# Hybrid decoder layer: two buffers for a head's K and Q, a freely issued second output tile, and 1/rms spread by transposes

## The chip, the cores and the metric

The kernel runs on one core of a Trainium2 chip, with TensorE (PE), VectorE (DVE), ScalarE (ACT), GpSimd (POOL) and SyncE (SP, which issues nearly all DMAs). The metric is the device time of one execution in microseconds. Beside the time of several runs there is one execution taken by the hardware profiler, whose instructions are shown here as "the trace"; times in it count from its first instruction.

## The reference

One decoder layer over 2048 positions of width 1024, all in float32, with a final RMSNorm:

```python
u = rmsnorm(h, norm_mix_w)
hq, hf, hi, hg, att = split(u @ w_in)
f = lb + (1 - lb) * sigmoid(hf)                  # 4 heads, key and value width 128
S_t = diag(f_t) S_{t-1} + (1 - f_t) v_t^T;  o_t = S_t^T q_t     # HGRN2
o_hg = rmsnorm(o, hg_norm_w) * silu(hg)
o_att = sliding_window_attention_with_sinks(att + b_attn)       # 8 query heads, 2 kv heads, window 128
h = h + concat(o_hg, o_att) @ w_out
v = rmsnorm(h, norm_ffn_w)
h = h + (silu(causal_conv(v @ w_gate)) * (v @ w_up)) @ w_down   # width 2816, conv of 3 taps
out = rmsnorm(h, final_norm_w)
```

rmsnorm multiplies by 1/sqrt(mean(x^2) + 1e-6), over the 1024 features of a position.

## The kernel before, in words

Features lie on the 128 partitions and positions along the free axis; the 2048 positions are worked in two halves of 1024 (`hf` = 0, 1), each 2 x 512 columns for one PSUM bank. A float32 product with a weight is made of three products of rounded parts, W_hi X_hi + W_hi X_lo + W_lo X_hi (float32r, one pass each; `split` and `prep` make the parts on ACT and DVE). `unit` is one such product of a 128-column block of weights with 8 blocks of X: 8 x 3 x 2 = 48 matmuls of 128x512. Products of float32 operands take two records each.

**Stages of a half.** The input norm and keys and values (kv); then a mixer of four HGRN2 heads (`hgrn`) woven with four attention pairs (`attend`); then `out_proj`, eight output tiles `pop` (d = 0 to 7) over the eight blocks of the mixer's output `M`; then the MLP (`gate_up`, `down`), whose products are saved by a Strassen-like scheme. All eight blocks enter every output tile, in the order 0, 4, 1, 5, 2, 6, 7, 3; blocks 7 and 3 are those of the last attention pair and the last head and come last.

**Order.** Each engine works through its own list of instructions in a fixed order. That order is written when the program is made: the generators of heads and attention are stepped by hand, which gives each instruction a priority, and a planner plays the program through on a modelled timeline, giving each engine the first instruction that is ready there. Tiles of one tag share a fixed number of buffers, and an instruction that needs a buffer waits until the last reader of the old tile is done. `tc.issue_after(ins)` keeps the instructions traced under it behind `ins` on that engine. `marks[m]` holds the last level product of level m, `marks["po"]` the last product of a head's output; `AFTER` says which output tiles are queued behind which mark. Here output tile 1 comes behind the last head's product of level m = 8 and tile 2 behind its po.

**A head.** `f` and `hq` are two units; `q` (named hg in the trace, its slot's name) is hq times 1/rms. K = 1 - f (L431) and Q = q f (L433). `pdiag` (L441) gives the diagonal of the score tile ST; seven levels m = 1 to 64 follow (`plev`, L469 for m < 32, L482 above): a product of Q with a copy G of K (L467), put into ST by L493, and then K and Q are multiplied by the decay of their neighbour (L475, L476, L485, L486), so that each level waits for the one before it. Then K is transposed (`pkn`, L511), `pu` and SS carry the state from block to block (L518, L522), `po` (L536, L537) is the output, with ST, Q and SS, `on` (L545) its norm, `pot` (L550) its transpose back, and the gate `g` is multiplied in. pdiag, plev, pkn, pu, po and pot all use the two PSUM banks of the tag "hg", and ST, Kn and `on` share two buffers of the tag "t4". Of attention pairs, `psc` are scores, `ppt` transposed probabilities, `po`/`pp` on DVE (L395) their masked copies, and `poT` (L403) the products with V; they use the two banks of "at". Units, gates and output tiles use four banks of "mm", output tile 2 those of "at".

The last two heads are stepped into each other: head 2's state and output are traced around the f and q units of head 3, and the levels of head 3 come behind them.

```python
            step(a2, h2, h3, a2, h2, a2)
            step(a3, h3, a3, h2, h3)
            for kt in (0, 4, 1, 5, 2, 6):
                M[kt] = split(mix[kt])
            step(h3, a3, h3, a3)
```

**Norms.** `Stats` adds up squares over the feature blocks in `acc`. `inverse` sums over the partitions by products with a column of ones (`pst`, L238), which leaves the sums of 128 positions in a column, takes 1/sqrt by `rsqrt` (a bit trick and three Newton steps on DVE, L152 to L162), and writes the diagonal of each column into `acc` (L242). `spread` (L252, `pinv`) multiplies that by a square of ones, so that each position's 1/rms stands on all partitions, and ACT copies it into `acc` (L255). The statistics are called invb, sums and acc in the trace after the tiles they lie in. At the very end the last half's first 512 columns are worked in two quarters, and the final products (L981) of both quarters are held behind the last instruction that `inverse` returns.

Of the kernel before, what the change touches and what calls it, by code (L numbers as in the profile page):

```python
# [8 lines left out]
F32 = mybir.dt.float32  # L9
# [4 lines left out]
ALU = mybir.AluOpType  # L14
# [3 lines left out]
P = 128  # L18
D = 1024
KT = D // P  # L20
S = 2048
HALF = 1024
# [3 lines left out]
HG = 4  # L26
# [7 lines left out]
QUADS = ["A11", "A12", "A21", "A22"]  # L34
PRODUCTS = [("P1", "A11", "B11"), ("P5", "S1", "T1"), ("P6", "S2", "T2"), ("P3", "S4", "B22"),
            ("P7", "S3", "T3"), ("P2", "A12", "B21"), ("P4", "A22", "T4")]
AFTER = {1: 8, 2: "po"}
LEVELS = [1, 2, 4, 8, 16, 32, 64]
NEG = -1.0e30
UT = 7  # L40
# [5 lines left out]
def hymba_layer(ctx: ExitStack, tc: tile.TileContext, a: dict, out: bass.AP):  # L46
    nc = tc.nc

    def pool(name, bufs=1, space=None, stack=ctx, **kw):
        if space is not None:  # L50
            kw["space"] = space
        return stack.enter_context(tc.tile_pool(name=name, bufs=bufs, **kw))
# [12 lines left out]
    def ps(kind, name):  # L65
        return spaces[kind].tile([P, 512], F32, tag=kind, name=name)
# [9 lines left out]
    ones = cp.tile([P, P], F32, name="ones")  # L76
# [3 lines left out]
    ident = cp.tile([P, P], F32, name="ident")  # L80
# [65 lines left out]
        nc.vector.tensor_scalar(C.omlb, C.lb, -1.0, 1.0, op0=ALU.mult, op1=ALU.add)  # L146


    def rsqrt(ss, n, scale, keep=None):

        ms = sp.tile([P, n], F32, tag=f"ms{n}", name="ms")
        nc.vector.tensor_scalar(ms, ss, scale, EPS, op0=ALU.mult, op1=ALU.add)  # L152
        y = sp.tile([P, n], F32, tag=f"y{n}{keep}", name="y")
        yi = y.bitcast(I32)
        nc.vector.tensor_scalar(yi, ms.bitcast(I32), 1, None, op0=ALU.logical_shift_right)
        nc.vector.tensor_scalar(yi, yi, -1.0, float(0x5F3759DF), op0=ALU.mult, op1=ALU.add)
        nc.vector.tensor_scalar(ms, ms, -0.5, None, op0=ALU.mult)
        t = sp.tile([P, n], F32, tag=f"t{n}", name="t")
        for _ in range(3):
            nc.vector.tensor_tensor(t, y, y, op=ALU.mult)  # L160
            nc.vector.tensor_tensor(t, t, ms, op=ALU.mult)
            nc.vector.scalar_tensor_tensor(y, t, 1.5, y, op0=ALU.add, op1=ALU.mult)  # L162
        return y

    def raw4(src):
# [5 lines left out]
    def prep(src, slots=False, parts=(slice(0, D),)):  # L171

        raw = raw4(None)
        hi, lo = [hp.tile([P, D], F32R, tag="m", name=f"w{t}", bufs=KT) if slots else
                  wp.tile([P, D], F32R, tag=t, name=f"w{t}", bufs=2) for t in ("hi", "lo")]
        for c in parts:
            nc.sync.dma_start(raw[:, c], src[:, c])
            nc.scalar.copy(hi[:, c], raw[:, c])  # L178
            nc.vector.tensor_tensor(lo[:, c], raw[:, c], hi[:, c].bitcast(F32), op=ALU.subtract)  # L179
        return hi, lo  # L180
# [34 lines left out]
    class Stats:  # L215
# [16 lines left out]
        def inverse(self, keep):  # L232

            n = self.acc.shape[-1]
            nt = n // P
            st = ps("hg", "pst")
            for c in range(nt):
                nc.tensor.matmul(st[:, c:c + 1], self.acc[:, c * P:(c + 1) * P], ones[:, 0:1],  # L238
                                 start=True, stop=True)
            rs = self.rs = rsqrt(st[:, 0:nt], nt, 1.0 / D, keep)  # L240
            dg = self.acc
            return nc.vector.tensor_tensor(dg.rearrange("p (c t) -> p c t", t=P),  # L242
                                    ident.unsqueeze(1).to_broadcast([P, nt, P]),
                                    rs.unsqueeze(2).to_broadcast([P, nt, P]), op=ALU.mult)

        def spread(self, bank=None):

            n = self.acc.shape[-1]
            w = min(n, 512)
            for b in range(n // w):  # L250
                pb = ps(aux[b % 2 if bank is None else bank], "pinv")[:, 0:w]
                nc.tensor.matmul(pb, ones, self.acc[:, b * w:(b + 1) * w], start=True, stop=True)  # L252
                if bank is not None:
                    return pb
                nc.scalar.copy(self.acc[:, b * w:(b + 1) * w], pb)  # L255
# [31 lines left out]
    def across(t, base, dims):  # L287

        v = t[:, :]
        return bass.AP(v.tensor, v.offset + base, [list(v.ap[0])] + dims)  # L290
# [126 lines left out]
    def hgrn(hf, h, X, invb, vs, WG, mix, p, fu=None):  # L417
# [9 lines left out]
            nc.vector.scalar_tensor_tensor(q[:, bs], qu[b], 128.0 ** -0.5, invb[:, bs], op0=ALU.mult, op1=ALU.mult)  # L427
        nc.vector.tensor_scalar(f, f, C.omlb[:, h:h + 1], C.lb[:, h:h + 1], op0=ALU.mult, op1=ALU.add)
        yield
        K = p.tile([P, HALF], F32, tag="K", name="K", bufs=1)  # L430
        nc.vector.tensor_scalar(K, f, -1.0, 1.0, op0=ALU.mult, op1=ALU.add)  # L431
        Q = p.tile([P, HALF], F32, tag="Q", name="Q", bufs=1)
        nc.vector.tensor_tensor(Q, q, f, op=ALU.mult)  # L433


        ST = p.tile([P, TT, P], F32, tag="t4", name="ST", bufs=2)
        for b in range(NB):
            pd = ps("hg", "pdiag")
            for i in range(4):
                c = slice((b * 4 + i) * P, (b * 4 + i + 1) * P)  # L440
                nc.tensor.matmul(pd[:, i * P:(i + 1) * P], K[:, c], q[:, c], start=True, stop=True)  # L441
            nc.vector.tensor_tensor(ST[:, 4 * b:4 * b + 4], pd.rearrange("p (i t) -> p i t", i=4),
                                    ident.unsqueeze(1).to_broadcast([P, 4, P]), op=ALU.mult)


        late = h == HG - 2

        def gate():
            gu = unit(WG.get(h, a["w_g"][h]), X, "g")
            s = p.tile([P, HALF], F32, tag="f", name="sg", bufs=2)  # L450
            t = p.tile([P, HALF], F32, tag="f", name="ug", bufs=2) if late else q
            for b, bs in halves():
                nc.vector.tensor_tensor(blocks(t[:, bs], b), blocks(gu[b]), blocks(invb[:, bs]), op=ALU.mult)
                nc.scalar.activation(s[:, bs], t[:, bs], AF.Sigmoid)
                if late:
                    nc.vector.tensor_tensor(q[:, bs], q[:, bs], t[:, bs], op=ALU.mult)
                nc.vector.tensor_tensor(q[:, bs], q[:, bs], s[:, bs], op=ALU.mult)

        F = f
        for m in LEVELS:  # L460
            nb = HALF // (2 * m)
            pl = ps("hg", "plev")
            if m < 32:
                n, nu = 64 // m, TT // 2
                far, near = [[512 - m, 2], [P, nu], [2 * m, n], [1, m]], [[512 + m, 2], [P, nu], [2 * m, n], [1, m]]
                G = p.tile([P, 512], F32, tag="G", name="G", bufs=2)
                nc.scalar.copy(across(G, 0, [[m, 2], [P, nu], [2 * m, n], [1, m]]), across(K, 0, near))  # L467
                for u in range(nu):
                    marks[m] = nc.tensor.matmul(across(pl, u * 64, [[256, 2], [1, 64]]), G[:, u * P:(u + 1) * P],  # L469
                                                across(Q, u * P + m, [far[0]] + far[2:]), start=True, stop=True)  # L470
                nf = P // m
                Kv, Qv = across(K, 0, near), across(Q, m, far)
                Fk = across(F, 1, [[4 * nf - 1, 2], [nf, nu], [2, n], [0, m]])
# [3 lines left out]
            else:  # L477
                Qv = Q.rearrange("p (b w m) -> p b w m", w=2, m=m)
                Kv = K.rearrange("p (b w m) -> p b w m", w=2, m=m)
                for c in range(TT):  # L480
                    for s0 in range(0, P, 2 * m):
                        nc.tensor.matmul(pl[s0:s0 + m, c * m:(c + 1) * m], K[:, c * P + s0:c * P + s0 + m],  # L482
                                         Q[:, c * P + s0 + m:c * P + s0 + 2 * m], start=True, stop=True)
                Fv = F.rearrange("p (b w) -> p b w", w=2)
# [22 lines left out]
        for b in range(NB):  # L507
            pk = ps("hg", "pkn")
            for i in range(4):
                c = slice((b * 4 + i) * P, (b * 4 + i + 1) * P)  # L510
# [3 lines left out]
        for b in range(NB):  # L514
            pu = ps("hg", "pu")
            for i in range(4):
                c = 4 * b + i
                marks["pu"] = nc.tensor.matmul(pu[:, i * P:(i + 1) * P], Kn[:, c], v[:, c], start=True, stop=True)  # L518
            for i in range(4):
                c = 4 * b + i  # L520
                prev = state[:, h] if c == 0 else SS[:, c - 1]
                nc.vector.scalar_tensor_tensor(SS[:, c], prev, F[:, c:c + 1], pu[:, i * P:(i + 1) * P],  # L522
                                               op0=ALU.mult, op1=ALU.add)
        yield
        g = q
        if h < HG - 2:
            gate()
            yield
        on = p.tile([P, TT, P], F32, tag="t4", name="on", bufs=2)
        ss = p.tile([P, TT], F32, tag="ss", name="ss", bufs=2)  # L530
        po = [ps("hg", "po") for _ in range(NB)]
        for c in range(TT):
# [3 lines left out]
            nc.tensor.matmul(o, ST[:, c], v[:, c], start=True, stop=False)  # L536
            marks["po"] = nc.tensor.matmul(o, Q[:, cs], prev, start=False, stop=True)  # L537
            nc.scalar.activation(on[:, c], o, AF.Square, accum_out=ss[:, c:c + 1])
        rs = rsqrt(ss, TT, 1.0 / P)
        if h == HG - 1:  # L540
            mix[h] = new_x()
# [5 lines left out]
        for b, bs in halves():  # L547
# [5 lines left out]
            else:  # L553
                nc.vector.scalar_tensor_tensor(blocks(g[:, bs]), blocks(pt, b), C.hgw, blocks(g[:, bs]),
                                               op0=ALU.mult, op1=ALU.mult)
# [48 lines left out]
    def out_proj(hf, M, p):  # L604
# [11 lines left out]
        for d in range(KT):  # L616
# [8 lines left out]
            if d >= len(W):  # L625
                W.append(prep(a["w_out"][d]))
            with tc.issue_after(marks[AFTER[d]].ins) if d in AFTER else ExitStack():
                o = unit(W[d], M, "pop", order, "at" if d == 2 else "mm", in_turn=d == KT - 1)
# [363 lines left out]
    for hf in range(NH):  # L992
        X, kv, invb, rs, f0 = nxt
        with ExitStack() as st:
            p = pool(f"mix{hf}", stack=st, reuse_waits="tile")
# [28 lines left out]
        with ExitStack() as st:  # L1024
            p = pool(f"ffn{hf}", stack=st, reuse_waits="tile")
# [65 lines left out]
```

## Time and profile before

| | |
|---|---|
| median of 3 runs | 2217.16 us (2214.91 to 2218.22) |
| the profiled execution | 2213.91 us, its span 2212.2 us |
| mean granted clock of TensorE | 0.995 |
| PE, PEld, DVE, ACT, POOL busy | 98%, 82%, 74%, 47%, 1% of the span |
| instructions | 29221 |
| DMA | 254.15 MB, 115 GB/s in the mean |

PEld is the loading of weights, which runs beside the matmuls. A matmul's record is longer than its share of a row of matmuls, since they are pipelined: the distance from start to start is the pace. A line such as L197 is that of a helper (`unit`); the tile's name says which product it is. In the rows of time, the bracket gives the idle time of the engine before the instruction and what ended it.

### The profile page before, as it was taken

How to read it: one execution, taken by the hardware profiler on the slowest of the kernel's cores; microseconds unless marked ns; L12 is line 12 of the kernel's file. 1: busy time of each engine (PE TensorE's matmuls, PEld its weight loads, DVE VectorE, ACT ScalarE, POOL GpSimd, SP SyncE). 2: the span in 40 equal slices, each digit the busy share in tenths (PEclk: the TensorE clock that was granted, in tenths of full speed). 3: DMA queues.
4: the chain of work that ended last, by engine and by line, in shares of the span. 5: the costliest groups of instructions: out<-in, count | busy, mean ns of one | idle time of the engine just before them, and what ended most of it. 6: DMA issues, size and time to landing. Idle time of an engine off the chain costs nothing.

```text
span 2212.2 us, 29221 instructions
## 1 busy us (share of the span) xinstructions
PE 2175.0 (98%) x11302; PEld 1822.3 (82%) x11302; DVE 1638.0 (74%) x2458; ACT 1049.3 (47%) x1825; POOL 14.4 (1%) x37
## 2 busy tenths in 40 slices
PE   8999998999999999999999999999999999999997
PEld 6988987778888888888889889878788888888887
DVE  6567567688887888775865666667878888887766
ACT  5445454454444445335725455535534444443353
POOL 2000000000000000000000000000000000000000
PEclk9999999999999999999999999999999999999999
DMA  4111112323333234964631111113232323359643
GB/s 154 39 29 39 29 29 77 108 83 93 113 100 115 87 128 145 376 230 159 203 124 38 30 29 39 59 37 136 64 125 86 125 85 119 95 194 393 220 130 128
DMA packets 89995, 254.15 MB, mean 115 GB/s; under 512 B 11008, under 2 KB 13184, under 8 KB 89856
## 3 DMA queue, kind: packets, MB, share of 16 engines
q1 hardware_dynamic: 87552, 251.17, 34.1%
q8 instruction: 88, 1.44, 0.3%
q10 hardware_dynamic: 2304, 1.12, 0.2%
q14 instruction: 51, 0.42, 0.1%
HBM read 195.10 MB, written 57.15 MB: 114 GB/s over the span
## 4 chain that ended last, share of the span: by engine, by line
PE 95%; DVE 3%; ACT 1%; DMA 1%; issue 0%; ACTq 0%; DVEq 0%
PE X L708 7%; PE X L709 7%; PE X L710 7%; PE pop L197 6%; PE q L197 4%; PE hq L197 4%; PE f L197 4%; PE pdx L890 4%; PE pdx L891 4%; PE Y L708 4%; PE pdx L892 4%; PE Y L710 4%; PE Y L709 4%; PE g L197 4%; PE pdy L891 3%; PE pdy L890 3%
## 5 line engine op out<-in xcount | busy, mean ns | idle before, releaser
L585 ACT CAST whi<-raw 128x1024 fp32r<-128x1024 f32 x88 | 92.7, 1053 | 109.7 <-PE X L709 68.8
L709 PE MATMUL X<-T,whi 128*128 128x512 f32 x352 | 137.4, 390 | 0.0
L708 PE MATMUL X<-T,whi 128*128 128x512 f32 x352 | 137.1, 389 | 0.0
L710 PE MATMUL X<-T,wlo 128*128 128x512 f32 x352 | 137.0, 389 | 0.0
L774 DVE SCALAR_TENSOR_TENSOR y<-ga,cw,y 128x1024 f32<-128x1024 f32 x88 | 112.4, 1277 | 28.2 <-ACT y L772 28.1
L714 ACT COPY u<-X 128x512 f32<-128x512 f32 x88 | 51.5, 585 | 122.3 <-PE X L710 122.2
L586 DVE TENSOR_TENSOR wlo<-raw,whi 128x1024 fp32r<-128x1024 f32 x88 | 107.0, 1216 | 0.0
L586 DVE TENSOR_TENSOR xld<-raw,xhd 128x1024 fp32r<-128x1024 f32 x72 | 80.5, 1129 | 18.9 <-ACT xhd L585 18.3
L178 ACT CAST whi<-raw 128x1024 fp32r<-128x1024 f32 (+2 forms) x61 | 62.9, 1035 | 65.9 <-PE hq L197 11.8
L585 ACT CAST xhd<-raw 128x1024 fp32r<-128x1024 f32 x72 | 69.7, 979 | 40.2 <-DMA raw<-act1T 14.4
L197 PE MATMUL pop<-XH,wlo 128*128 128x512 f32 x256 | 83.3, 391 | 0.7 <-DVE wlo L179 0.7
L197 PE MATMUL pop<-XL,whi 128*128 128x512 f32 x256 | 84.0, 392 | 0.0
L197 PE MATMUL pop<-XH,whi 128*128 128x512 f32 x256 | 82.9, 396 | 0.4 <-ACT XH L208 0.2
L179 DVE TENSOR_TENSOR wlo<-raw,whi 128x1024 fp32r<-128x1024 f32 (+2 forms) x61 | 72.9, 1199 | 13.9 <-ACT whi L178 13.9
L708 PEld LDWEIGHTS X<-T,whi 128*128 128x128 f32 x352 | 66.1, 188 | 14.0 <-ACT u L714 0.3
L710 PEld LDWEIGHTS X<-T,wlo 128*128 128x128 f32 x352 | 66.1, 188 | 13.9 <-issue 0.2
L709 PEld LDWEIGHTS X<-T,whi 128*128 128x128 f32 x352 | 66.1, 188 | 13.8 <-issue 0.2
L890 PE MATMUL pdx<-xhd,hid 128*128 128x512 f32 x192 | 74.4, 391 | 1.0 <-ACT hid L585 1.0
L891 PE MATMUL pdx<-xld,hid 128*128 128x512 f32 x192 | 74.8, 390 | 0.0
L708 PE MATMUL X<-T,Sh 128*128 128x512 f32 x176 | 69.0, 392 | 5.2 <-ACT s L714 5.2
L892 PE MATMUL pdx<-xhd,lod 128*128 128x512 f32 x192 | 73.7, 389 | 0.0
L578 PE MATMUL pvv<-whi,XL 128*128 128x256 f32 x256 | 73.2, 287 | 0.0
(363 smaller groups left out, 6544.5 us busy)
## 6 DMA issues: line engine op xcount, KB each, us to landing
wr<-in_w_down SPq DMA_DIRECT2D x90, 512.0 KB, 5.2
raw<-in_w_gate SPq DMA_DIRECT2D x44, 512.0 KB, 3.7
raw<-in_w_up SPq DMA_DIRECT2D x44, 512.0 KB, 3.6
raw<-act0T SPq DMA_DIRECT2D x20, 512.0 KB, 5.6
raw<-act1T SPq DMA_DIRECT2D x20, 512.0 KB, 5.3
act0B<-y SPq DMA_DIRECT2D x33, 256.0 KB, 2.4
act1B<-y SPq DMA_DIRECT2D x33, 256.0 KB, 2.4
raw<-in_w_out SPq DMA_DIRECT2D x16, 512.0 KB, 3.7
```

The costliest lines, as they stand in the source:

```text
L179: nc.vector.tensor_tensor(lo[:, c], raw[:, c], hi[:, c].bitcast(F32), op=ALU.subtract)
L197: nc.tensor.matmul(o[b], w, x[:, bs], start=f, stop=l)
L578: nc.tensor.matmul(o[:, 0:256], xl[:, t], hi[:, c], start=False, stop=False)
L585: nc.scalar.copy(h, src)
L586: (eng or nc.vector).tensor_tensor(l, src, h.bitcast(F32), op=ALU.subtract)
L708: nc.tensor.matmul(o, wh[:, ws], xh, start=i == 0 and not more, stop=False, skip_group_check=more)
L709: nc.tensor.matmul(o, wh[:, ws], xl, start=False, stop=False, skip_group_check=more)
L710: nc.tensor.matmul(o, wl[:, ws], xh, start=False, stop=i == 3, skip_group_check=more)
L774: nc.vector.scalar_tensor_tensor(y, g[:, w:w + HALF], C.cw[:, ft, w:w + 1], y, op0=ALU.mult, op1=ALU.add)
L890: nc.tensor.matmul(o, wh[:, i, c], ah[:, i, cols], start=f, stop=False, skip_group_check=more)
L891: nc.tensor.matmul(o, wh[:, i, c], al[:, i, cols], start=False, stop=False, skip_group_check=more)
L892: nc.tensor.matmul(o, wl[:, i, c], ah[:, i, cols], start=False, stop=l, skip_group_check=more)
```

## The change

Three edits. K and Q of a head get two buffers each (L430, L432). `AFTER` loses its entry for output tile 1, so that its products may be issued at any time. `inverse` no longer writes the diagonal and returns the last Newton step; `spread` transposes, for each 128 positions, the column of 1/rms read as a square (its column broadcast along the free axis with step 0), which gives the same square as before. The two lines on `late` say the same as before for four heads.

```diff
-AFTER = {1: 8, 2: "po"}
+AFTER = {2: 'po'}
...
+    made = []
+
     def rsqrt(ss, n, scale, keep=None):
...
-            nc.vector.scalar_tensor_tensor(y, t, 1.5, y, op0=ALU.add, op1=ALU.mult)
+            made.append(nc.vector.scalar_tensor_tensor(y, t, 1.5, y, op0=ALU.add, op1=ALU.mult))
         return y
...
-            rs = self.rs = rsqrt(st[:, 0:nt], nt, 1.0 / D, keep)
-            dg = self.acc
-            return nc.vector.tensor_tensor(dg.rearrange("p (c t) -> p c t", t=P),
-                                    ident.unsqueeze(1).to_broadcast([P, nt, P]),
-                                    rs.unsqueeze(2).to_broadcast([P, nt, P]), op=ALU.mult)
+            self.rs = rsqrt(st[:, 0:nt], nt, 1.0 / D, keep)
+            return made[-1]
...
-                nc.tensor.matmul(pb, ones, self.acc[:, b * w:(b + 1) * w], start=True, stop=True)
+                for c in range(w // P):
+                    i = b * w // P + c
+                    nc.tensor.transpose(pb[:, c * P:(c + 1) * P], self.rs[:, i:i + 1].to_broadcast([P, P]), ident)
...
-        K = p.tile([P, HALF], F32, tag="K", name="K", bufs=1)
+        K = p.tile([P, HALF], F32, tag="K", name="K", bufs=2)
         nc.vector.tensor_scalar(K, f, -1.0, 1.0, op0=ALU.mult, op1=ALU.add)
-        Q = p.tile([P, HALF], F32, tag="Q", name="Q", bufs=1)
+        Q = p.tile([P, HALF], F32, tag="Q", name="Q", bufs=2)
...
-        late = h == HG - 2
+        late = h in (2,)
...
-        if h < HG - 2:
+        if not late and h < HG - 1:
             gate()
```

## The prediction

> **What bounds the kernel now.** I read the page first (its busy shares and the chain that ended last), then busy time by stage, then the order of time on TensorE (PE) and VectorE (DVE) in the one stage where PE stops.
>
> ```profile
> span 2212.2 us, 29221 instructions
> ...
> PE 2175.0 (98%) x11302; PEld 1822.3 (82%) x11302; DVE 1638.0 (74%) x2458; ACT 1049.3 (47%) x1825; POOL 14.4 (1%) x37
> ...
> PE 95%; DVE 3%; ACT 1%; DMA 1%; issue 0%; ACTq 0%; DVEq 0%
> ```
>
> PE works in 2175.0 of 2212.2 us and carries 95% of the chain. Time can come from two places only: less work on PE, or the 37 us in which it stands still. The table by stage (stretch, its length, then busy time and instruction count of PE, PEld, DVE, ACT and POOL, then the granted clock, DMA share, GB/s) says where it stands.
>
> ```profile
> 60.00:340.00 280.00, 280.00 (x1909) 244.82 (x1908) 180.31 (x348) 140.88 (x347) 0.00 (x0) 1.00 0.13 38
> 340.00:412.00 72.00, 65.09 (x413) 53.68 (x412) 49.42 (x94) 29.80 (x81) 0.00 (x0) 0.98 0.21 66
> ...
> 500.00:1100.00 600.00, 599.49 (x2641) 494.93 (x2641) 479.99 (x582) 279.63 (x369) 0.00 (x0) 1.00 0.47 160
> ...
> 1432.00:1506.00 74.00, 69.11 (x436) 56.51 (x435) 51.10 (x97) 30.52 (x83) 0.00 (x0) 0.98 0.26 84
> ...
> 2185.00:2212.20 27.20, 15.28 (x116) 13.96 (x115) 13.28 (x52) 4.56 (x8) 0.00 (x0) 0.81 0.25 88
> ```
>
> Heads 0 to 2 (60 to 340) and the MLP (500 to 1100) leave PE no idle time worth naming, so work taken from PE there is time gained and lateness elsewhere costs nothing. Where the last head's levels meet the first output tiles, PE idles 72.00 - 65.09 = 6.91 us in the first half and 74.00 - 69.11 = 4.89 us in the second. Two of the three edits act there. PE in order of time (start, length, instruction, count, and in brackets the idle time before it and who ended it):
>
> ```profile
> 332.26 1.03 PE L550 MATMUL pot<-ident,on 128*128 128x128 f32 x8
> ...
> 337.84 1.95 PE L441 MATMUL pdiag<-hg,K 128*128 128x128 f32 x16
> ...
> 350.31 1.07 PE L469 MATMUL plev<-Q,G 128*128 128x128 f32 x8
> 351.63 1.09 PE L392 MATMUL ppt<-ident,sc 128*128 128x128 f32 x8 [0.25 <-DVE sc L365]
> 353.74 1.16 PE L469 MATMUL plev<-Q,G 128*128 128x128 f32 x8 [1.02 <-DVE Q L476]
> 354.65 0.71 PE L197 MATMUL pop<-XH,whi 128*128 128x512 f32 x2
> 358.50 1.41 PE L403 MATMUL poT<-po,V 128*64 128x128 f32 x7 [3.14 <-DVE pp L395]
> ...
> 363.67 1.05 PE L469 MATMUL plev<-Q,G 128*128 128x128 f32 x8
> ...
> 370.95 1.05 PE L469 MATMUL plev<-Q,G 128*128 128x128 f32 x8
> ...
> 1450.97 0.98 PE L403 MATMUL poT<-po,V 128*64 128x128 f32 x3 [2.33 <-DVE pp L395]
> ```
>
> In the first half the hole is 0.25 + 1.02 + 3.14 = 4.41 us between the second level product (350.31, m = 2) and poT; in the second half its main piece is 2.33 us. The hole also slows what follows. In the chain in order of time (start, length, what):
>
> ```profile
> 43.54 1.72 PE pinv L252 x4
> ...
> 300.76 1.67 PE poT L403 x26
> ...
> 359.00 3.25 PE poT L403 x26
> ...
> 364.73 6.38 PE pop L197 x28
> ...
> 1450.97 3.98 PE poT L403 x32
> ...
> 1469.89 1.90 PE poT L403 x32
> ```
>
> The same 26 poT products take 3.25 us right behind the hole and 1.67 elsewhere, the 32 of the second half 3.98 against 1.90: another 1.58 and 2.08 us, in the two stretches whose granted clock is 0.98 in the mean and not 1.00. So the holes are worth 4.41 + 1.58 = 5.99 and 2.33 + 2.08 = 4.41 us, 10.4 together.
>
> **The change part by part. First, the spread by transposes.** The 1/rms columns are spread in `spread` (L252) by a full product of ones with a diagonal that DVE builds (L242). That diagonal goes, and four transposes take the place of each 512-wide product.
>
> ```profile
> L252 PE MATMUL pinv<-invb,ones x22: 379/592/797, 43.4 to 2203.4; 128*128 128x512 f32 x18, 128*128 128x256 f32 x4
> ...
> L252 PE MATMUL pinv<-sums,ones x4: 590/590/592, 1108.9 to 1125.2; 128*128 128x512 f32 x4
> ```
> ```profile
> L550 PE MATMUL pot<-ident,on 128*128 128x128 f32 x64 | 8.6, 274 | 0.0
> ```
>
> The code calls the 512-wide product 11 times (2 for the input norm and 2 for the MLP norm in each half, 2 + 1 for the final norm), and the trace has 18 + 4 = 22 records of it: each is two passes. Four passes take 1.72 us (the pinv row of the chain), 0.43 each, 0.86 a call. A transpose is one record: 64 of pot are 4 heads x 2 halves x 8. Eight of them last 1.03 us and one alone 0.274, so the next starts after (1.03 - 0.27) / 7 = 0.108 us; four are 0.43. Each call saves 0.43 us, 11 calls 4.7 us, all on PE and in stages where PE does not wait. The trace shows no weight load from a column broadcast with step 0; its nearest rows are the pot loads, whose weights are read with step 1, and I take their pace. Were nothing to overlap, 44 x 0.274 = 12.1 us would stand against 22 x 0.43 = 9.5, a loss of 2.6: the bounds are -4.7 and +2.6, and I take -4.7, because pot, with new weights for every product as here, keeps the pace of 0.108 in the same program.
>
> The Trainium skill, "TensorE: Matmul & The Clock Gate", Part 4 (PE-mode transpose), speaks against this edit: it gives about 275 ns for a transpose in a kernel and says that transposing does not bring up the clock. By that figure 44 of them cost 12.1 us, the loss just named. The trace agrees on the single one (274 ns) and not on a row of them (0.108 us each).
>
> The nine products that DVE loses lie beside busy PE, but for the last:
>
> ```profile
> L242 DVE TENSOR_TENSOR invb<-ident,y x7: 425/1222/1226, 37.1 to 2202.3; 128x1024 f32<-128x1024 f32 x4, 128x256 f32<-128x256 f32 x2, 128x512 f32<-128x512 f32 x1
> ```
> ```profile
> 2202.33 0.42 DVE L242 TENSOR_TENSOR invb<-ident,y 128x256 f32<-128x256 f32 x1
> 2202.68 5.38 DVE L981 TENSOR_TENSOR h<-h,pinv 128x256 f32<-128x256 f32 x16
> 2202.81 1.22 PE L252 MATMUL pinv<-invb,ones 128*128 128x256 f32 x2 [2.33 <-DVE invb L242]
> ```
>
> At the end DVE runs L242 and then the 16 final products without a break: -0.35 us (2202.33 to 2202.68). The spread of the last quarter, done at 2204.03, is wanted only by the ninth product (2202.68 + 8 x 5.38 / 16 = 2205.4), so its shorter transposes gain nothing. No DMA is moved.
>
> **Second, two buffers for K and Q.** DVE in the same stretch:
>
> ```profile
> 292.12 0.69 DVE L431 TENSOR_SCALAR K<-f 128x1024 f32<-128x1024 f32 x1
> ...
> 322.02 1.23 DVE L433 TENSOR_TENSOR Q<-hg,f 128x1024 f32<-128x1024 f32 x1 [3.50 <-PE po L537]
> ...
> 328.02 1.28 DVE L545 TENSOR_TENSOR on<-po,y 128x512 f32<-128x512 f32 x2
> ...
> 339.43 1.22 DVE L209 TENSOR_TENSOR XL<-att,XH 128x1024 fp32r<-128x1024 f32 x1
> ...
> 340.89 1.27 DVE L442 TENSOR_TENSOR ST<-pdiag,ident 128x512 f32<-128x512 f32 x2
> ...
> 361.20 0.68 DVE L476 TENSOR_TENSOR Q<-Q,F 128x512 f32<-128x512 f32 x1
> ...
> 364.89 0.68 DVE L476 TENSOR_TENSOR Q<-Q,F 128x512 f32<-128x512 f32 x1
> ...
> 1415.18 1.22 DVE L433 TENSOR_TENSOR Q<-hg,f 128x1024 f32<-128x1024 f32 x1 [2.15 <-PE po L537]
> ```
> ```profile
> 322.00:366.00 44.00, 41.95 (x75) 0.96 0.29 90
> ```
>
> Q of the last head does wait 3.50 and 2.15 us for the last po product of head 2. With a second buffer it is made before that. But K stood ready at 292.12, and pdiag, which reads K and hg and not Q, still came at 337.84. Two other things hold the levels: the two "hg" PSUM banks, which head 2's po has until L545 (328.02) and its pot until it is read after 332.26, and the two "t4" buffers, which head 2's ST and `on` have until its po has read them, so that the eviction into the last head's ST (L442, 340.89) cannot start sooner. Both stay. What goes is 1.2 us of Q from the stretch 322 to 366, where DVE works 41.95 of 44.00 us and which ends the hole on PE: between 0 and 2 x 1.2 = 2.4 us. I take 0, because the next edit fills the same hole. K gains nothing: it was not waited for.
>
> **Third, the second output tile is free.** Its 48 products (8 blocks of the mixer's output, 6 each) were queued behind the level product of m = 8 (363.67). Four blocks are split by 340.65 (L209 at 339.43 is the fourth); at 0.228 us (6.38 / 28) their 24 products are 5.5 us of work that is ready when PE stops for 4.41 and 2.33 us. The two "mm" banks they need are free once the last gate is read. If they fill the holes, the slow poT behind them goes too. What loses its cover then: after 363.67 those products stood between the levels. The m = 16 product, ready at 364.89 + 0.68 = 365.57, began only at 370.95, 5.4 us late behind pop. So taking 5.5 us away there brings the chain of the levels forward by about as much; the next late thing is the last attention head's softmax, whose products cannot follow all the way. No wait and no DMA is added. Bounds: 0 (all given back later) to -10.4. I take three quarters, -7.8, since most of what moves was itself delaying the chain. The order is written by a planner from a modelled timeline, so the placing is not exact.
>
> **Sum.** -4.7 - 0.35 - 0 - 7.8 = -12.9 us. The profiled execution took 2213.9 us (its span is 2212.2), which gives 2201.0; it lies 3.3 under the median of the runs shown, 2217.2, so I forecast 2204.3 as a median.
>
> **The rivals.**
> - *Given back.* The tile fills the hole, and PE then idles as long between 363 and 392, where DVE has room and the last softmax and head set the pace. For it: PE has little else there. Against it: the 5.4 us at 370.95. Only the first edit is left: 2217.2 - 5.1 = 2212.1.
> - *The levels do start early.* The planner puts pdiag and the levels of the last head ahead of 322, and PE's idle time in both stretches goes, 6.91 + 4.89 = 11.8 us, with the slow poT, 3.7: 2217.2 - 5.1 - 15.5 = 2196.6. Against it: the banks.
> - *Slower: the tile is queued ahead of the levels.* The planner takes DVE for later than it is (as at m = 16) and lays the 24 products before the products of m = 1 to 4; every level moves back 5.5 us, and later nothing is left to cover it. Two halves cost 11.0, less the 5.1: 2223.1. It decides when the third level product (353.74 now) comes later than the hole is long, after 358.1. Against it: that product waits for DVE now, not for pop.
> - *Transposes do not overlap.* +2.6 in place of -4.7, the rest as forecast: 2217.2 + 2.6 - 0.35 - 7.8 = 2211.7. The rule quoted above says so; pot's pace speaks against it.
>
> **How the numbers follow.** Forecast 0.60, given back 0.18, early levels 0.10, slower 0.07, no overlap 0.05. About 0.2% (4.4 us) is what a measurement can tell from no change, so faster begins at 2212.8. Faster: 0.60 + 0.10, 0.04 of no overlap and a bit over half of given back (it stands 0.7 us inside), less some of the forecast that falls short: 0.78. Slower 0.08, same 0.14. The range runs from the early levels to a little above given back, 2196 to 2214; the forecast alone would have 2199 to 2210.
>
> **What would show it.** First edit: 48 transposes at L252's place, 0.11 us apart, no L242, and the final products 0.35 us nearer to the end of the last Newton step. Second: L433 before 305 and 1400 with no wait for po; pdiag still near 337. Third: pop between 350 and 358 in place of 3.14 and 2.33 us of idle time, poT behind it at 1.7 us for 26, and the m = 16 product near 366. The prediction is wrong if PE's idle time in the 72 us from 340 is not under 4 us in the first half, or if the transposes stand 0.27 us apart.

## The result and the profile after

The changed kernel takes 2201.49 us (median of 4 runs, 2199.78 to 2202.70) against 2217.18 before; the ratio is 0.993, 95% interval 0.9913 to 0.9947. That is 15.7 us faster, where 12.9 were forecast. Beside later experiments it was timed once more: 2200.82 us, ratio 0.9928 (0.9916 to 0.994).

In its profiled execution the span is 2198.0 us, 14.2 less. From the page:

```profile
span 2198.0 us, 29255 instructions
...
PE 2164.7 (98%) x11324; PEld 1816.3 (83%) x11324; DVE 1629.8 (74%) x2449; ACT 1048.2 (48%) x1825; POOL 12.0 (1%) x37
...
PE 94%; DVE 3%; ACT 1%; DMA 1%; issue 0%; DVEq 0%; SPq 0%; ACTq 0%
```

PE is busy 10.3 us less and idle 3.9 us less (33.3 for 37.2), and still carries the chain. Part of the "busy" that went was the slow poT, which counts as work. The two stretches that the prediction looked at, by the table of stages (the first is laid 7 us earlier, since its end has come forward by that, the second 12):

```profile
333.00:405.00 72.00, 69.46 (x450) 57.25 (x448) 53.69 (x100) 33.52 (x86) 0.00 (x0) 1.00 0.27 82
1420.00:1494.00 74.00, 70.36 (x455) 57.24 (x454) 53.50 (x99) 32.55 (x86) 0.00 (x0) 1.00 0.27 88
```

The columns are those of the prediction's table. PE idles 2.54 and 3.64 us there, before 6.91 and 4.89, and its clock is 1.00 throughout. PE in order of time in the first of them:

```profile
334.71 1.05 PE L442 MATMUL pdiag<-hg,K 128*128 128x128 f32 x8
...
350.07 1.07 PE L470 MATMUL plev<-Q,G 128*128 128x128 f32 x8
...
352.24 0.71 PE L199 MATMUL pop<-XL,whi 128*128 128x512 f32 x2
...
356.89 1.05 PE L470 MATMUL plev<-Q,G 128*128 128x128 f32 x8
...
359.92 0.43 PE L404 MATMUL poT<-po,V 128*64 128x128 f32 x2
...
363.80 1.16 PE L470 MATMUL plev<-Q,G 128*128 128x128 f32 x8
...
366.04 1.05 PE L470 MATMUL plev<-Q,G 128*128 128x128 f32 x8
```

Output products, with transposes and one level product between them, run from 350.89 up to poT, where 4.41 us of idle time stood; not one row between 349 and 366 has a bracket. The poT products are woven with other work now, and a single one lasts 0.27 us (0.42 behind the hole before). The third level product (356.89) waits for nothing; the fifth, m = 16, begins at 366.04 and not at 370.95. DVE in time order shows the last head's Q: made at 292.49, where it had waited for po until 322.02.

```profile
292.49 1.16 DVE L434 TENSOR_TENSOR Q<-hg,f 128x1024 f32<-128x1024 f32 x1
```

The spread, by its line and in time order; in the second fence DVE at the end:

```profile
L253 PE MATMUL pinv<-ident,y x48: 270/272/475, 41.7 to 2188.8; 128*128 128x128 f32 x48
...
41.70 1.04 PE L253 MATMUL pinv<-ident,y 128*128 128x128 f32 x8
```
```profile
2188.36 0.16 DVE L164 SCALAR_TENSOR_TENSOR y<-t,y 128x2 f32<-128x2 f32 x1
2188.44 5.38 DVE L982 TENSOR_TENSOR h<-h,pinv 128x256 f32<-128x256 f32 x16
```

48 transposes; eight last 1.04 us, so (1.04 - 0.27) / 7 = 0.11 each, and weights read from a column with step 0 show no other pace than pot's (0.108). The final products start 0.08 us after the start of the last Newton step; L242 no longer stands between.

### The profile page after: what moved, and what is told of

Read it like the earlier page. It is cut to its first block, busy times and chain, and to the rows that moved or that the text cites. A ratio compares the mean times of both kernels' runs of the same rounds, so it can differ in the third digit from the quotient of the medians.

```text
span 2198.0 us, 29255 instructions
## 1 busy us (share of the span) xinstructions
PE 2164.7 (98%) x11324; PEld 1816.3 (83%) x11324; DVE 1629.8 (74%) x2449; ACT 1048.2 (48%) x1825; POOL 12.0 (1%) x37
## 4 chain that ended last, share of the span: by engine, by line
PE 94%; DVE 3%; ACT 1%; DMA 1%; issue 0%; DVEq 0%; SPq 0%; ACTq 0%
PE X L709 7%; PE X L711 7%; PE X L710 7%; PE pop L199 7%; PE hq L199 4%; PE g L199 4%; PE q L199 4%; PE f L199 4%; PE pdx L891 4%; PE pdx L892 4%; PE pdx L893 4%; PE Y L709 4%; PE Y L710 4%; PE Y L711 4%; PE pdy L892 3%; PE pdy L891 3%
## 5 line engine op out<-in xcount | busy, mean ns | idle before, releaser
L586 ACT CAST xhd<-raw 128x1024 fp32r<-128x1024 f32 x72 | 69.6, 977 | 43.7 <-DMA raw<-act0T 15.5
L181 DVE TENSOR_TENSOR wlo<-raw,whi 128x1024 fp32r<-128x1024 f32 (+2 forms) x61 | 72.9, 1200 | 12.9 <-ACT whi L180 12.8
```

Source lines behind the costliest of these rows:

```text
L586: nc.scalar.copy(h, src)
```

## The experiments

All kernels start from the kernel before or the changed one; ratios are to the kernel before, from runs on the same chip.

**The three edits one by one (e1 to e4).** Each edit alone, and the first and third together, with the others put back as they were:

```diff
# e2: the edit of AFTER alone;  e3: the two edits of bufs alone;  e1: neither, only the spread;
# e4: the spread and the edit of AFTER, with bufs=1
-AFTER = {1: 8, 2: "po"}
+AFTER = {2: 'po'}
...
-        K = p.tile([P, HALF], F32, tag="K", name="K", bufs=1)
+        K = p.tile([P, HALF], F32, tag="K", name="K", bufs=2)
...
-        Q = p.tile([P, HALF], F32, tag="Q", name="Q", bufs=1)
+        Q = p.tile([P, HALF], F32, tag="Q", name="Q", bufs=2)
```

> The spread by transposes alone; K and Q keep one buffer, output tile 1 stays behind the level product of m = 8. Theory: 11 calls save 0.43 us each on PE and the tail 0.35, so 5.1 us less than before (ratio about 0.9977), and the holes before poT stay at about 3 and 2.3 us. Rival (the gain in heads 0 to 2 of the changed kernel, 1.3 and 1.0 us that no step of the prediction names, comes from the diagonal's products gone from VectorE): 7.5 us less, and the first output tile begins 2.2 us earlier than before where it should be 0.9.

> Output tile 1 free alone; the norms as before, K and Q with one buffer. Theory: the holes are filled by this edit by itself: idle time of TensorE before poT under 1 us in both halves, poT at 1.7 us for 26, 7 us less than before (ratio 0.9968). Rival 1 (the second buffer of Q fills the hole, the free tile only goes along): the holes stay, 0 to 2 us less. Rival 2 (given back): holes gone, but idle time from 363 to 392 grows by as much, 0 to 1 us less.

> Two buffers for K and Q alone. Theory: the second Q loses its wait of 3.50 and 2.15 us on VectorE but pdiag of the last head stays near 337 (it waits for PSUM banks and for ST), so 0 to 2.4 us less than before, most likely nothing on the holes. Rival (Q's wait was what held VectorE back in the stretch that ends the hole): holes smaller by 1 us or more in each half and 3 us or more less; if the 2.4 us gained in heads 0 to 2 of the changed kernel are this edit's, they show here between 47 and 290 and between 1131 and 1374.

> The changed kernel with one buffer each for K and Q: spread by transposes and the free tile together. Theory: the sum of the two, 12 us less than before (ratio 0.9946), within 2.5 us of the changed kernel. Rival (the three edits need each other, the free tile pays only when Q is early): 5 to 7 us less.

| | median us | ratio (95%) | us less, from the ratio |
|---|---|---|---|
| e1 spread alone | 2213.66 | 0.9986 (0.9977 to 0.9995) | 3.1 |
| e2 free tile alone | 2207.63 | 0.9962 (0.9950 to 0.9975) | 8.4 |
| e3 K and Q alone | 2216.60 | 0.9998 (0.9989 to 1.0007) | 0.4 |
| e4 spread and free tile | 2202.07 | 0.9936 (0.9923 to 0.9948) | 14.2 |
| all three | 2201.49 | 0.9930 (0.9913 to 0.9947) | 15.5 |

By the times, the free tile brings most, the spread the rest, and the buffers nothing that can be told from zero: e4, without them, is within 0.6 us of the changed kernel. In e2 the holes are gone though Q has one buffer. In e3, where Q has two, they do not go but move: in the first half four waits, none longer than 1.26 us, make 3.45 us where 4.41 stood, and the clock stays at 1.00; in the second half the wait before poT grows from 2.33 to 3.13 us, and the clock is 0.95. By stage, and PE's waits of the second half in time order, e3:

```profile
340.00:412.00 72.00, 66.14 (x423) 53.79 (x422) 47.99 (x91) 28.63 (x74) 0.00 (x0) 1.00 0.26 83
1432.00:1506.00 74.00, 67.20 (x417) 54.27 (x416) 48.30 (x92) 29.38 (x80) 0.00 (x0) 0.95 0.21 70
```

```profile
1442.40 1.09 PE L394 MATMUL ppt<-ident,sc 128*128 128x128 f32 x8 [0.24 <-DVE sc L367]
1444.52 1.16 PE L471 MATMUL plev<-Q,G 128*128 128x128 f32 x8 [1.02 <-DVE Q L478]
1449.27 0.98 PE L405 MATMUL poT<-po,V 128*64 128x128 f32 x3 [3.13 <-DVE pp L397]
```

and e2, whose longest wait up to poT in the first half is 0.48 us:

```profile
366.69 1.13 PE L471 MATMUL plev<-Q,G 128*128 128x128 f32 x8 [0.29 <-DVE Q L478]
368.76 1.26 PE L394 MATMUL ppt<-ident,sc 128*128 128x128 f32 x8 [0.48 <-DVE sc L385]
```

One instruction in each half, the first lo product of output tile 3, serves as a milestone. PE in time order, from before, e2 and the changed kernel in turn:

```profile
409.52 0.74 PE L197 MATMUL pop<-XH,wlo 128*128 128x512 f32 x2 [0.37 <-DVE wlo L179]
1502.33 0.73 PE L197 MATMUL pop<-XH,wlo 128*128 128x512 f32 x2 [0.38 <-DVE wlo L179]
```
```profile
404.71 0.74 PE L199 MATMUL pop<-XH,wlo 128*128 128x512 f32 x2 [0.39 <-DVE wlo L181]
1495.04 0.74 PE L199 MATMUL pop<-XH,wlo 128*128 128x512 f32 x2 [0.38 <-DVE wlo L181]
```
```profile
402.37 0.73 PE L199 MATMUL pop<-XH,wlo 128*128 128x512 f32 x2 [0.40 <-DVE wlo L181]
1489.91 0.73 PE L199 MATMUL pop<-XH,wlo 128*128 128x512 f32 x2 [0.38 <-DVE wlo L181]
```

e2 is 4.8 us ahead at the first, 7.3 at the second; the changed kernel 7.2 and 12.4. Part of that is the start of the program, which differs by 1.2 us between two profiles of the same kernel (the first hq product begins at 46.03 in the changed kernel and at 47.24 in e9, the same kernel profiled again). Counted from a product ahead of the mixer, profiles of the same kind agree to 0.1 us (e8, e9 and e10 are described below; e8 and e9 have two buffers, e10 has one):

| us | before | free tile, one buffer | free tile, two buffers |
|---|---|---|---|
| first hq product to the first milestone | 362.3 | 358.2 (e2, e4 and e10) | 356.3 (changed, e8), 356.4 (e9) |
| first kv product of the second half to the second milestone | 401.1 | 398.2 (e2), 396.5 (e4, e10: four spread calls lie in it) | 396.2 to 396.4 (changed, e8, e9: four spread calls) |

So the free tile by itself brings 4.2 + 2.9 = 7.1 us in the two mixers, four spread calls 1.8 (0.44 each), and the second buffers another 1.8 in the first half and 0.2 in the second, which the times are too coarse to show. Without the free tile (e3) the buffers gain 2.7 us in the first half and lose 2.8 in the second. DVE in time order shows how they gain, e4 with one buffer and then the changed kernel:

```profile
320.53 1.22 DVE L434 TENSOR_TENSOR Q<-hg,f 128x1024 f32<-128x1024 f32 x1 [3.50 <-PE po L538]
...
326.52 1.28 DVE L546 TENSOR_TENSOR on<-po,y 128x512 f32<-128x512 f32 x2
```
```profile
325.14 1.29 DVE L546 TENSOR_TENSOR on<-po,y 128x512 f32<-128x512 f32 x2
```

With one buffer, the last head's Q stands on DVE between head 2's po and the norm that ends head 2 (L546). With two it was made long before, and, counted from the first hq product (45.69 in e4, 46.03 in the changed kernel), the norm comes 1.7 us sooner. With the norm, the hg banks come free sooner, and pdiag of the last head begins 288.7 us after the first hq product, where it is 290.7 in every profile of a kernel with one buffer. In the second half pdiag comes 1.1 us later with two buffers, and why is open.

The changed kernel's last hq product is earlier by 1.3 and 1.0 us than the rest explains; e1 was to test whether that comes from the spread. It comes with the buffers: e3 shows it too (1.3 us in the first half), e1 and e4 don't. It is no gain by itself: PE has no idle time from 60 to 340 to save, in the changed kernel either,

```profile
60.00:340.00 280.00, 280.00 (x1910) 244.50 (x1909) 180.03 (x348) 143.39 (x361) 0.00 (x0) 1.00 0.13 39
```

so what moves is which work stands ahead of the last hq.

e1 gave 3.1 us of the 5.1 expected; 5.1 is at the very end of its interval (1.1 to 5.1). Its rival, 7.5, is ruled out. On top of the free tile the spread brings 2207.63 - 2202.07 = 5.6, with an interval of about 2.8 us to either side of each of the two. e1's profile shows what took some back. The first mixer, in which no spread call lies behind the first hq product, is 0.7 us longer than before by the count above (363.0), and the second is shorter by 0.6 (400.6), where four calls should make it 1.7. There is also a longer wait where the last MLP stage begins, and a longer stretch of half clock behind a stall in the second half:

```profile
892.96 0.50 PE L891 MATMUL pdx<-xhd,hid 128*128 128x512 f32 x1 [1.36 <-ACT hid L586]
...
1563.60:1570.60 7.00, 7.00 (x22) 5.85 (x21) 5.26 (x9) 1.86 (x3) 0.00 (x0) 0.51 0.13 49
```

Whether these are in all of its runs was not seen, so that difference stays open.

**Output tile 2 free too (e5).**

```diff
-AFTER = {2: 'po'}
+AFTER = {}
```

> The changed kernel with output tile 2 freed from its mark too. In the changed kernel its 36 products (8.2 us) cover the last head's way from po to its transpose back (384.7 to 393). Theory (cover used early is missed where nothing else is ready): TensorE idles 4 to 8 us there in each half and the kernel is 5 to 14 us slower than the changed one, near 2210. Rival (filler moved forward brings everything behind it forward, as it did for tile 1): within 2 us of the changed kernel, near 2201.

2215.01 us, ratio 0.999 (0.9981 to 0.9999): 13.5 us slower than the changed kernel. The theory holds. PE in time order and by stage:

```profile
398.71 1.84 PE L551 MATMUL pot<-ident,on 128*128 128x128 f32 x8 [3.70 <-DVE on L546]
401.20 1.65 PE L199 MATMUL pop<-XH,whi 128*128 128x512 f32 x3 [0.64 <-ACT XH L559]
...
378.00:408.00 30.00, 25.57 (x128) 20.98 (x127) 12.51 (x35) 7.25 (x23) 0.00 (x0) 0.89 0.13 44
1473.00:1503.00 30.00, 24.15 (x120) 19.29 (x117) 13.24 (x35) 6.82 (x23) 0.00 (x0) 0.89 0.12 41
```

With tile 2 used up early, po comes late (8.2 us later than in the changed kernel in the first half, counted from the first hq product) and then nothing is ready between po and pot: 4.4 and 5.9 us idle, with the clock at 0.89 in the mean. The mark on tile 2 is worth 13 us, the one on tile 1 cost 7 to 8.

**The levels in other banks (e6).**

```diff
-            pd = ps("hg", "pdiag")
+            pd = ps("mm" if h == HG - 1 else "hg", "pdiag")
...
-            pl = ps("hg", "plev")
+            pl = ps("mm" if h == HG - 1 else "hg", "plev")
```

> The changed kernel with the last head's pdiag and level products in the four mm banks instead of the two hg banks; nothing else is changed. Tests what held its levels back. Theory (the PSUM banks that head 2's po and pot hold, not Q and not ST): pdiag comes before 325 instead of near 337, about as soon as head 2's po is through; but the gates' products need the same mm banks, so the levels run without cover and TensorE idles 8 to 20 us between 310 and 340: slower than the changed kernel, 2205 to 2225. Rival (ST or K and Q hold them): pdiag stays behind pot and the time within 2 us.

2216.16 us, ratio 0.9993 (0.9984 to 1.0002). PE in time order and by stage:

```profile
309.94 0.39 PE L442 MATMUL pdiag<-hg,K 128*128 128x128 f32 x2
...
316.85 1.07 PE L470 MATMUL plev<-Q,G 128*128 128x128 f32 x8
...
310.00:343.00 33.00, 26.39 (x206) 22.43 (x205) 27.89 (x62) 23.36 (x68) 0.00 (x0) 0.90 0.05 17
```

With other banks pdiag begins at 309.94, inside head 2's po, where it stood at 334.71: with two buffers for K and Q, it was the hg banks that held the levels. And early levels are no gain as such: the products of the last head's gate, which would cover them, begin only at 338.72, PE idles 6.6 us (8 to 20 were expected) at a clock of 0.90, and 14.7 us are lost against the changed kernel. That the gate waits for the same mm banks was reasoned from the code, and no row shows it.

**Each transpose twice (e7).**

```diff
-                for c in range(w // P):
+                for c in [*range(w // P)] * 2:
```

> The changed kernel with every transpose of the spread done twice into the same place, 48 more transposes. Theory (0.108 us each in a row): 44 more on the path cost 4.7 us, near 2206, and the records stand 0.11 us apart. Rival (a transpose costs its whole duration of 0.27 us): 12 us more, near 2213.5. If the transposes were hidden anyway: no change.

2211.27 us, ratio 0.9981 (0.9971 to 0.9990), 9.8 us above the changed kernel: between the two, and nearer to the rival's 12. In time order and by stage:

```profile
41.37 1.91 PE L253 MATMUL pinv<-ident,y 128*128 128x128 f32 x16
...
889.37 0.78 PE L891 MATMUL pdx<-xhd,hid 128*128 128x512 f32 x1 [2.62 <-ACT hid L586]
...
462.60:466.20 3.60, 3.01 (x7) 2.43 (x8) 3.60 (x6) 1.60 (x5) 0.00 (x0) 0.53 0.50 146
```

Sixteen transposes last 1.91 us, again 0.11 each, and all 96 have a median of 0.273: 44 more of them on the path make 4.8 us, as the theory has it. The profile is 10.3 us longer. Most of the rest is in two places: a wait of 2.62 us (0.51 in the changed kernel) where the last MLP stage of the first half begins, with 3.6 us at a clock of 0.53 behind it, and another such stretch behind the stall before S2 in the first half (462.60), where the changed kernel's profile has none; 2.1 + 1.7 + 1.7 = 5.5 us. Why the wait grew is open. So the total is no measure of the transpose; the records are.

**S1 ahead of S2 in the first pair (e8).** The one stall over 1 us that the changed kernel has left between its start and the final norm stands before S2, 2.62 us in each half.

```diff
+        if first:
+            prod(Y, "S1", "T1")
+            s5 = out(Y, "s5")
+            prod(X, "S2", "T2", True)
+            u2 = out(X, "u2")
+            prod(Y, "S4", "B22", True)
+            evac(0, 1, Y, u2)
+            prod(X, "S3", "T3", True)
...
-            then = {"S2": lambda: hs.inverse("h"), "S4": lambda: (hs.spread(), flush())} if pr == 0 else {}
+            then = {"S2": lambda: hs.inverse("h"), "A22": lambda: (hs.spread(), flush())} if pr == 0 else {}
```

> The changed kernel with another order of products in the first pair of the MLP only: A11, A12, S1, S2, S4, S3, A22 instead of A11, A12, S2, S1, S3, S4, A22, and the MLP norm's spread ahead of A22. In every kernel so far TensorE stands still 2.6 us in each half before S2, which adds onto the bank that ScalarE has yet to copy, and half a clock window (3.4 us at half clock) sometimes follows. Theory: S1 covers the copy, both stalls go, 3 to 8 us less than the changed kernel, near 2196. Rival (VectorE is what is late there, splitting the operands, and a new stall comes at S3, A22 or the spread): within 3 us of the changed kernel.

2196.67 us, ratio 0.9901 (0.9886 to 0.9916): 4.8 us below the changed kernel's median and the fastest of all. The changed kernel, in time order and by stage:

```profile
462.63 0.50 PE L709 MATMUL X<-T,Sh 128*128 128x512 f32 x1 [2.62 <-ACT s L715]
...
1550.17 0.79 PE L709 MATMUL X<-T,Sh 128*128 128x512 f32 x1 [2.62 <-ACT s L715]
...
455.00:500.00 45.00, 42.05 (x196) 34.42 (x195) 39.02 (x64) 25.88 (x41) 0.00 (x0) 1.00 0.20 64
1540.00:1590.00 50.00, 47.38 (x214) 39.12 (x213) 43.22 (x71) 28.50 (x46) 0.00 (x0) 0.97 0.20 60
```

and e8:

```profile
455.00:500.00 45.00, 44.80 (x209) 36.74 (x208) 40.35 (x67) 28.18 (x45) 0.00 (x0) 1.00 0.19 60
1540.00:1590.00 50.00, 49.80 (x231) 40.90 (x230) 45.14 (x74) 30.31 (x50) 0.00 (x0) 1.00 0.23 74
```

Idle time of 2.95 and 2.62 us is 0.20 and 0.20, and the clock is 1.00. A part comes back further on: the wait where the last MLP stage begins is 1.31 and 1.29 us in the two halves, where it was 0.51. In time order, e8's second half:

```profile
1970.57 0.50 PE L902 MATMUL pdx<-xhd,hid 128*128 128x512 f32 x1 [1.29 <-ACT hid L586]
```

**Once more, and e8 with one buffer (e9, e10).** e9 is the changed kernel as it is; e10 is e8 with `bufs=1` for K and Q.

> The changed kernel once more, beside the kernel before and the next one on the same chip. Theory: 2201.5 within 2 us, as in its own runs. Half-clock windows of 3.4 us behind the two 2.6 us stalls before S2 should come and go from one profile to the next, since the program is the same: none to two of them ahead of the end.

> The kernel with S1 ahead of S2 in the first pair, with one buffer each for K and Q again. Theory (the second buffers are worth nothing): the same as with two, 2196.7 within 2 us, and 4 to 7 us less than the changed kernel. Rival (the second Q is worth its 1.2 us on VectorE twice, or more by the order it allows): 2199 or above.

e9: 2200.82, ratio 0.9928 (0.9916 to 0.994), with one stretch of half clock ahead of the end, behind the stall of the second half as in the first profile. e10: 2197.73, ratio 0.9917 (0.9904 to 0.9931), 3.1 us below e9, where 4 to 7 were expected, and 1.1 above e8. Three pairs (e3 with before, e4 with the changed kernel, e10 with e8) now put the second buffers at 0.3 to 1.1 us by their medians and at 0.4 to 3.5 by their ratios; the intervals of each pair overlap, so no pair tells them from zero. By the traces they bring 2.0 us in the two mixers once the tile is free, in e10 against e8 as in e4 against the changed kernel.

## Why the prediction was right, point by point

- **The place.** "The holes" before poT were where the time was: the free tile alone takes them and brings 8.4 us by the times, and the poT behind them is no longer slow.
- **The first term, -4.7, and the tail, -0.35.** The pace of 0.108 us, read from pot, is 0.11 in the changed kernel and in e7, and the four calls in the second half's mixer bring 0.44 us each, where 0.43 was reckoned. The Trainium skill's figure of about 275 ns ("TensorE: Matmul & The Clock Gate", Part 4) is again the duration of one record (0.272), not the price of one in a row. On top of the free tile the times agree with the whole 5.1 us (5.6); alone the spread brought 3.1, and that difference is open.
- **The second term, 0, is the step that was wrong.** "The next edit fills the same hole" left out what the buffer does ahead of the hole. Q was early (292.49), as said, and the banks did hold pdiag (e6), but Q had also stood on DVE ahead of the norm that frees these banks, so pdiag came 2.0 us sooner in the first half. With the free tile the second buffers are worth 1.8 + 0.2 = 2.0 us by the traces, inside the stated bounds of 0 to 2.4 and near their upper end. That ST, too, was held by head 2 was argued only; in e6 it did not keep pdiag and the first level (316.85) from running.
- **The third term, -7.8, is a little too large.** By the traces the free tile alone brings 4.2 us in the first half, of the 5.99 that the hole and its slow poT were reckoned at, and 2.9 in the second, of 4.41: 7.1 of 10.4, so that "three quarters" was about two thirds. The level product of m = 16 came at 366.04, where "near 366" was said.
- **The sum.** At the second milestone the changed kernel is 12.4 us ahead: 0.3 from the start of the program, 3.4 from the eight spread calls ahead of it, 7.1 from the tile and 2.0 from the buffers, less about 0.4 that is given back between the two mixers. The three calls behind it and the tail make 1.65 more, which is the 14.2 us of the two profiles within 0.2. The further 1.5 us of the medians is inside the interval. A term too small by 2.0 and one too large by 0.7 stood against each other, so that the forecast came as near as it did is in part luck.
- **The rivals.** "Given back" needs PE to idle more between 363 and 392; it idles 1.8 us in the same work, before 1.9. "Slower" was to be decided by a third level product after 358.1: it stands at 356.89, only just short of it, and 4.3 us later than before when both are counted from the first hq product. Output products now stand ahead of that level, as this rival has it, but the hole is gone and m = 16 comes 3.8 us sooner by the same count. That filler can be spent too early is shown for tile 2 (e5). "Transposes do not overlap" fails by the pace of 0.11 us. "Early levels" fails at its cover, not only at the banks (e6): with the banks it is 14.7 us slower and not faster.

## What to carry to other kernels

Work that is ready at any time is worth as much as the idle time that it is laid into, and a fixed mark on it should be set where nothing else is ready: here the mark of one tile cost 7 to 8 us and that of the next, a few lines of time later, saves 13. Before giving a waiting operand a second buffer, look for the next thing that its consumer needs (here PSUM banks), for what would cover the work if it did come early, and for what the late operand stands in front of on its own engine: here, in the first half, the buffer paid not by the early operand but by the norm that no longer queued behind it. Price an operation by the distance from start to start in a row of its kind, not by the length of one record.

## What the runs showed of the hardware that was not expected

A wait of 2 to 4 us on PE often costs more than itself (not each time): behind it the granted clock stands at 0.53 for 3.6 us, in some profiles for 7.0 at 0.51. Before, behind the two holes and the stall before S2; the changed kernel behind that stall in the second half; e4 behind the same stall in the first:

```profile
358.60:362.20 3.60, 3.50 (x29) 2.93 (x28) 3.60 (x6) 0.62 (x1) 0.00 (x0) 0.53 0.00 0
1451.00:1454.60 3.60, 3.60 (x31) 3.01 (x32) 3.60 (x5) 0.62 (x1) 0.00 (x0) 0.53 0.19 18
1563.60:1567.20 3.60, 3.60 (x14) 2.99 (x12) 3.60 (x7) 0.62 (x1) 0.00 (x0) 0.53 0.31 122
```
```profile
1550.20:1553.80 3.60, 3.60 (x9) 2.88 (x10) 3.60 (x6) 1.58 (x3) 0.00 (x0) 0.53 0.49 146
```
```profile
465.40:472.40 7.00, 7.00 (x22) 5.81 (x21) 5.32 (x9) 1.86 (x3) 0.00 (x0) 0.51 0.14 54
```

By an estimate from these rows each stretch of 3.6 us costs (1 - 0.53) x 3.6 = 1.7 us, and the same stall of 2.62 us has it in one half or kernel and not in another, which may be part of why medians of so like kernels differ by 2 us. The Trainium skill ("TensorE: Matmul & The Clock Gate", Part 1) tells of half clock in free-running windows of 3.4 us after an idle one, which agrees with the rate and the length of these stretches, though none of the waits ahead of them was as long as such a window. The same page's advice to keep gaps under about 3 us ("Why this matters for your kernels") does not suffice here, since 2.33 and 2.62 us were enough.
